# Another order of the seven products in both down projections, with half of one product's loads on the queue of the sums

## The chip, the core and the metric

The kernel runs on one core of one Trainium2 chip. The metric is device time in microseconds (us): the median of three runs of the kernel before is 1141.16 us (1140.47 to 1141.63). The profile is one execution, taken by the hardware profiler. Its engines are called PE (matrix multiply) and PEld (its weight load), DVE (VectorE), ACT (ScalarE), POOL (GpSimd) and SP (SyncE). SP, POOL and ACT also issue transfers (DMAs), which run on 16 DMA engines. Times inside the profile count from the start of its span.

## What is computed

The program is a two-layer decoder trunk on one sequence of 512 tokens with 1024 features, all in float32. Each layer is a mixer (attention in the first layer, a gated short convolution in the second) and a gated MLP, each behind an RMS norm and with a residual add. The change concerns the end of the MLP, its down projection:

```
SEQ = 512; D_MODEL = 1024; D_FF = 2816
def conv_ffn(h, norm_g, w_up, conv_w, w_down):
    xn = rms_norm(h, norm_g)
    u = causal_dwconv(xn @ w_up, conv_w)
    g, val = u[..., :D_FF], u[..., D_FF:]
    return (jax.nn.silu(g) * val) @ w_down
...
for layer in range(2):
    h = h + (attention_mixer(...) if layer == 0 else short_conv_mixer(...))
    h = h + conv_ffn(h, ffn_norm[layer], ffn_w_up[layer], ffn_conv[layer], ffn_w_down[layer])
```

So a down projection multiplies a 512 x 2816 matrix by a 2816 x 1024 matrix, once per layer.

## The kernel before

**The seven products.** `mlp` cuts the activations, the weights and the result of the down projection into two by two blocks and computes seven block products in place of eight. Their names are `p1 p7 p6 p2 q4 q5 p3`, and `PHASES` holds the order in which they run; this text calls them stage 1 to stage 7 by their place in it. One product runs over half of D_FF, which is 11 tiles of 128 rows. `GROUPS` cuts these into six chunks of 2, 2, 2, 1, 2 and 2 tiles. A chunk's weights are 512 KB, or 256 KB for the one of a single tile. One step of the program is one chunk, so a layer has 42 steps.

**Where a product's weights come from.** Two products take a block of the weights as it is: `p2` and `p3` load it into one of three buffers called `raw` (a plain load, on SP's queue). The other five take sums of blocks, and the additions are done by transfers. A transfer on POOL's queue with `accum_op` adds a block from memory to what lies in a tile. There are two chains of six tiles, one tile for each chunk:

- the first chain holds block (0,0) for `p1` (a plain load), and a later sum adds block (0,1) to it for `q5`;
- the second chain holds block (0,1) (a plain load), to which a first sum adds (1,1) for `p7`, a second adds (0,0) for `p6` and a third adds (1,0) for `q4`.

A sum may start only when the earlier content of its tile has been read. POOL issues its transfers in the order of the program, and while one waits, those behind it wait too. The tiles of the chains lie in tiles that the up projection has used, and carry their names: those of the first chain are `X_chain`, `Y_chain` and `p1_hi`/`p1_lo_chain`, those of the second `p7_hi`/`p7_lo_chain`, `q5_hi`/`q5_lo_chain` and `q4_hi`/`q4_lo_chain` for chunks 0 to 5. The number behind `chain` is the chunk, the next one the layer. The profile leaves leading numbers out and shows them as `p_hi_chain`, `q_lo_chain` and so on.

**The split.** A float32 product is made of three matmuls with a high and a low half of each factor. For each chunk ACT writes the high half of the weights (`whi`, L250) and DVE the low half (`wlo`, L251), each with three buffers. The same is done for the chunk's activations (`act`, L946 and L950 or L952). `weights` calls `fetch`, which loads and splits chunks two steps ahead of the one that PE works on; so a split is also held back by PE, which must have left the buffer of three chunks before. The load of a chunk on SP is issued as soon as its `raw` buffer is free.

**PE.** `step` does the matmuls of a chunk (L1505): 24 of 256 columns in the first layer and 12 of 512 columns in the second (half as many for the chunk of one tile), 132 and 66 in a stage. The accumulators A, T, R and B are two PSUM banks each; R starts as a negative copy of A.

**Other work of the stages.** DVE adds blocks of the activations in place for later products (L1407, L1409, L1411, from `operand`). `tasks` spreads adds into the residual (`join`, L1442), stores (`store`, L1447) and, in the first layer, the start of the next norm (`feed`) over the steps. The trailing slots of the up projection run in stage 1, and in the second layer the residual is transposed back in stages 2 and 3 (L1431).

Of the kernel before, what the change touches and what calls it, by code (L numbers as in the profile page):

```python
# [25 lines left out]
P = 128  # L26
# [27 lines left out]
def trunk(  # L54
# [158 lines left out]
    def want(dram, k0, nk, c0, n, *more):  # L213
        wanted.append((dram, k0, nk, (c0, n) + more))

    def want_sum(place, nk, n, *blocks):

        wanted.append((place, nk, n, blocks))

    def load(i):  # L220

        hi = wp.tile([P, CHUNK], F32R, tag="whi", name=f"whi{i}", bufs=3)
        lo = wp.tile([P, CHUNK], F32R, tag="wlo", name=f"wlo{i}", bufs=3)
        if callable(wanted[i][0]):
            place, nk, n, blocks = wanted[i]
            raw = place()
            if raw is None:
                raw = wp.tile([P, CHUNK], F32, tag="raw", name=f"raw{i}")
            v = raw[:, 0:nk * n].rearrange("p (k c) -> p k c", c=n)
            for (dram, k0, c0), fresh in blocks:  # L230
                src = dram[k0 * P:(k0 + nk) * P, c0:c0 + n].rearrange("(k p) c -> p k c", p=P)
                if fresh:
                    nc.sync.dma_start(v, src)
                else:
                    tc.keep_in_program_order(nc.gpsimd.dma_start(v, src, accum_op=ALU.add))
# [12 lines left out]
        def part(a, b):  # L248
            at_ = slice(a * n, b * n)
            return (act.activation(hi[:, at_], raw[:, at_], AF.Copy),  # L250
                    dve.tensor_tensor(lo[:, at_], raw[:, at_], f32(hi[:, at_]), op=ALU.subtract))  # L251
        halve[i] = part, nk
        return [t[:, 0:nk * n].rearrange("p (k c) -> p k c", c=n) for t in (hi, lo)]
# [37 lines left out]
    class Norm:  # L291
# [2 lines left out]

        def __init__(self, name, base):
            self.name, self.base = name, base
            self.row, self.held = None, []
            self.acc = own.tile([P, S], F32, tag="nrow", name=f"nacc_{name}", bufs=1) if name != "n0" else None

        def feed(self, f, src):  # L300
# [7 lines left out]
            dve.scalar_tensor_tensor(lo, src, g, f32(hi), op0=ALU.mult, op1=ALU.subtract)  # L308

        def squares(self, f, src):  # L310
            if f == 0:
# [118 lines left out]

    want_ffn(0, 2 * CLASSIC)

    def products(acc, w):
        for k in range(ND):
            yield mm3(acc, (w[0][:, k, :], w[1][:, k, :]), hs(k), k == 0, k == ND - 1)

    def project(acc, w):
        run(products(acc, w))
# [781 lines left out]
    def conv_seven(norm, mp):  # L1220
# [108 lines left out]
        accs = []  # L1329
        for j in range(8):  # L1330
            accs.append(bank("bbbbaabb"[j]))
            for _ in products(accs[-1], weights()):
                up.work_off(SHARE)
            if j in (1, 3):
                chores.append(input_(j // 2, *accs[j - 1:]))
            if j == 3:
                chores.append(prepare())
            if j >= 4:
                chores.insert(0, gate(j - 4, accs[j]))
            if j == 5:  # L1340
# [16 lines left out]
    def mlp(layer, norm, mp):  # L1357
        blocks, slots = up_seven(layer, norm, mp)
        acts, c1, c2 = {}, {}, {}
        PHASES = ("p1", "p7", "p6", "p2", "q4", "q5", "p3")  # L1360
        steps = [(p, g) for p in range(7) for g in range(len(GROUPS))]
        act_tags = [f"{n}_{i}" for n in ("p6", "p2") for i in ("hi", "lo")]

# [15 lines left out]
        def block(kh, ch, k0, fresh):  # L1379
            return (ffn_w_down[layer], kh * HF + k0, ch * 512), fresh  # L1380

        for name in PHASES:
# [14 lines left out]
        def operand(i):  # L1397
            if i >= len(steps):
                return
            p, g = steps[i]  # L1400
            k0, nk = GROUPS[g]
            name, sign = SOURCE[PHASES[p]]
            t = acts[i] = mp.tile([P, 2, 2, HT], F32R, tag=act_tags[i % 4], name=f"act{layer}_{i}")
            halves_to(t[:, 0, 0:nk, :], t[:, 1, 0:nk, :], blocks.block(name, k0, nk), sign)
            a, b, c, d = (blocks.block(n, k0, nk) for n in "abcd") if p in (1, 3, 4) else (None,) * 4
            if p == 1:
                dve.tensor_tensor(b, b, c, op=ALU.add)  # L1407
            elif p == 3:
                dve.tensor_tensor(a, b, a, op=ALU.subtract)  # L1409
            elif p == 4:  # L1410
                dve.tensor_tensor(b, b, d, op=ALU.add)  # L1411
# [8 lines left out]
        trail = slots[n_up:]  # L1420

        A, T, R, B = ([] for _ in range(4))
        home = {"p1": (A, "a", True), "p7": (T, "b", True), "p6": (R, "b", False), "p2": (A, None, False), "q5": (R, None, False),
                "p3": (B, "a", True), "q4": (T, None, False)}
        both, SUB = range(2), ALU.subtract
        kept = {}
# [17 lines left out]
        def store(i, ch, tb, acc, cuts=(0, 512)):  # L1444
# [6 lines left out]
        tasks = {  # L1451
            "p1": trail,
            "p7": [],
            "p6": [lambda b=b: join(1, 1, b, T[b], SUB) for b in both],
            "p2": [lambda b=b: join(1, 0, b, R[b], SUB) for b in both],
            "q4": [lambda b=b: done(0, 0, b, A[b]) for b in both],
            "q5": [lambda b=b: done(1, 0, b, T[b]) for b in both],
            "p3": [lambda b=b, fn=fn, i=i: fn(i, 1, b, R[b]) for b in both for fn, i in ((done, 1), (join, 0))],
        }
        after_ = None  # L1460
        if layer:
            residuals = [lambda q=q: residual_in(*q) for q in
                         ((1, 1, 0), (1, 1, 1), (1, 0, 0), (1, 0, 1), (0, 0, 0), (0, 0, 1), (0, 1, 0), (0, 1, 1))]
            tasks["p7"] += [None, None] + residuals[0:4]
            tasks["p6"] += residuals[4:]
        else:
            after_ = Norm("n2", 16)

            def feed(f):
                if f == 0:  # L1470
                    hs_open(1)
                after_.feed(f, h[:, f, :])
            tasks["q5"] += [lambda f=f: feed(f) for f in range(4)]

        def finish(b):
            if layer:
                store(0, 1, b, B[b], cuts=(0, 384, 512) if b else (0, 512))
                return
            join(0, 1, b, B[b])
            for f in (4 + 2 * b, 5 + 2 * b):  # L1480
                feed(f)

        todo = []
        for i, (p, g) in enumerate(steps):
            name, (k0, nk) = PHASES[p], GROUPS[g]
            acc, tag, fresh = home[name]
            if g == 0:
                todo.extend(tasks[name])
                if tag:
                    acc.extend(bank(tag) for _ in both)  # L1490
                if name == "p6":
                    for tb in both:
                        act.activation(R[tb], A[tb], AF.Copy, scale=-1.0)

# [14 lines left out]
            if i < late:  # L1509
# [78 lines left out]
```

## Time and profile before

| what | value |
|---|---|
| median of three runs | 1141.16 us |
| the profiled execution | 1140.43 us, its span 1138.5 us |
| mean granted clock of PE in the span | 0.998 |
| PE busy | 1123.4 us (99%) |
| DVE busy | 959.3 us (84%) |
| ACT busy | 669.3 us (59%) |
| POOL busy | 136.0 us (12%) |
| down projection of the first layer (L1505) | 504.09 to 621.29 us |
| down projection of the second layer (L1505) | 1017.11 to 1134.62 us |

A busy PE is not PE at its peak, since matmuls are pipelined; what tells of lost time is that the same number of matmuls takes longer in one stage than in another. Idle time of an engine that nobody waits for costs nothing. In the list of transfers a row gives the issue; the time to landing stands in a view of its own.

### The profile page before, as it was taken

To read this page: it belongs to the slowest core of one execution; us is meant where nothing else is said; L and a number is where in the kernel's file an instruction comes from. 1 tells how busy PE (TensorE), PEld (TensorE's weight loads), DVE (VectorE), ACT (ScalarE), POOL (GpSimd) and SP (SyncE) were. 2 spreads that over 40 slices of the span, in tenths; PEclk is the share of its full clock that TensorE was granted. 3 is DMA by queue.
4 is the path that set the end of the run, shared out by engine and by line. 5 is a ranking of instruction groups with operands and counts; after the bars stand their busy time and mean duration, and the time that the engine had idled before them with its cause. 6 is when DMAs were issued, how large, how long until landed. Compare 5 with 4: busy or idle time off the path is not lost.

```text
span 1138.5 us, 19066 instructions
## 1 busy us (share of the span) xinstructions
PE 1123.4 (99%) x7547; PEld 1006.6 (88%) x7547; DVE 959.3 (84%) x1453; ACT 669.3 (59%) x999; POOL 136.0 (12%) x150
## 2 busy tenths in 40 slices
PE   8999999999999999999999999999999999999998
PEld 6888787878889999999999899988889999998776
DVE  5787888887899899989788889865898898989775
ACT  7556576755545667676475455543445767676553
POOL 4000000000012111014400001000012111014400
PEclk9999999999999999999999999999999999999999
DMA  6412212022366877689944555543275867699952
GB/s 192 112 38 75 56 39 73 26 87 75 110 178 120 179 170 162 173 247 190 213 101 143 145 144 133 113 118 98 83 192 117 191 161 162 172 246 190 206 144 83
DMA packets 161080, 155.31 MB, mean 136 GB/s; under 512 B 6396, under 2 KB 136492, under 8 KB 160992
## 3 DMA queue, kind: packets, MB, share of 16 engines
q1 hardware_dynamic: 124256, 106.94, 30.6%
q0 software_dynamic: 36576, 47.10, 25.8%
q8 instruction: 59, 0.97, 0.3%
q14 instruction: 29, 0.24, 0.1%
q10 hardware_dynamic: 160, 0.07, 0.0%
HBM read 149.10 MB, written 2.10 MB: 133 GB/s over the span
## 4 chain that ended last, share of the span: by engine, by line
PE 86%; DVE 8%; DMA 2%; ACT 2%; issue 1%; SPq 0%; DVEq 0%; ACTq 0%
PE psb L997 25%; PE psa L997 10%; PE psb L1505 10%; PE psb L271 6%; PE psb L272 6%; PE psb L273 6%; PE psa L1505 5%; PE psa L273 4%; PE psa L272 4%; PE psa L271 4%; DVE wlo L251 2%; DMA raw<-in_ffn_w_down 2%; PE psb L645 1%; PE psa L741 1%; DVE rest L686 1%
## 5 line engine op out<-in xcount | busy, mean ns | idle before, releaser
L250 ACT ACTIVATE whi<-raw 128x1024 fp32r<-128x1024 f32 (+2 forms) x97 | 100.0, 1033 | 110.2 <-PE psb L272 32.0
L251 DVE TENSOR_TENSOR wlo<-raw,whi 128x1024 fp32r<-128x1024 f32 (+2 forms) x97 | 115.2, 1189 | 41.4 <-ACT whi L250 39.4
L997 PE MATMUL psb<-p_hi,wlo_p 128*128 128x256 f32 x384 | 108.3, 282 | 0.6 <-DVE wlo_p L950 0.6
L997 PE MATMUL psb<-p_lo,whi_p 128*128 128x256 f32 x384 | 108.1, 281 | 0.0
L997 PE MATMUL psb<-p_hi,whi_p 128*128 128x256 f32 x384 | 107.8, 281 | 0.0
L271 PE MATMUL psb<-hs_a,whi 128*128 128x512 f32 x256 | 104.6, 409 | 0.0
L273 PE MATMUL psb<-hs_a,wlo 128*128 128x512 f32 x256 | 101.3, 397 | 0.0
L997 PEld LDWEIGHTS psb<-p_hi,wlo_p 128*128 128x128 f32 x384 | 72.2, 188 | 0.8 <-DVE wlo_p L950 0.8
L997 PEld LDWEIGHTS psb<-p_hi,whi_p 128*128 128x128 f32 x384 | 72.8, 190 | 0.0
L997 PEld LDWEIGHTS psb<-p_lo,whi_p 128*128 128x128 f32 x384 | 72.2, 188 | 0.0
L997 PE MATMUL psa<-p_lo,whi_p 128*128 128x256 f32 x256 | 72.0, 281 | 0.0
L997 PE MATMUL psb<-q_hi,whi_q 128*128 128x256 f32 x256 | 72.0, 281 | 0.0
L997 PE MATMUL psb<-q_lo,whi_q 128*128 128x256 f32 x256 | 72.0, 281 | 0.0
L997 PE MATMUL psb<-q_hi,wlo_q 128*128 128x256 f32 x256 | 72.0, 281 | 0.0
L997 PE MATMUL psa<-p_hi,wlo_p 128*128 128x256 f32 x256 | 72.0, 281 | 0.0
L997 PE MATMUL psa<-p_hi,whi_p 128*128 128x256 f32 x256 | 71.8, 281 | 0.0
L1505 PE MATMUL psb<-act,whi 128*128 128x256 f32 x352 | 63.0, 282 | 0.4 <-DVE act L950 0.4
L380 DVE SCALAR_TENSOR_TENSOR uv<-yv,taps,uv 128x511 f32<-128x511 f32 (+1 forms) x88 | 62.5, 745 | 0.2
L380 DVE SCALAR_TENSOR_TENSOR ug<-yg,taps,ug 128x511 f32<-128x511 f32 (+1 forms) x88 | 62.0, 743 | 0.3 <-ACT ug L377 0.3
L271 PEld LDWEIGHTS psb<-hs_a,whi 128*128 128x128 f32 x256 | 48.4, 189 | 10.7 <-issue 1.2
L273 PEld LDWEIGHTS psb<-hs_a,wlo 128*128 128x128 f32 x256 | 48.1, 188 | 10.9
L1505 PE MATMUL psb<-whi,act 128*128 128x512 f32 x176 | 57.4, 399 | 0.1
(453 smaller groups left out, 3654.9 us busy)
## 6 DMA issues: line engine op xcount, KB each, us to landing
raw<-in_attn_w_in SPq DMA_DIRECT2D x24, 512.0 KB, 4.0
raw<-in_ffn_w_up SPq DMA_DIRECT2D x24, 512.0 KB, 3.9
raw<-in_ffn_w_down SPq DMA_DIRECT2D x20, 512.0 KB, 8.1
X<-in_ffn_w_up SPq DMA_DIRECT2D x16, 512.0 KB, 4.7
W<-in_ffn_w_up SPq DMA_DIRECT2D x16, 512.0 KB, 6.7
Y<-in_ffn_w_up SPq DMA_DIRECT2D x16, 512.0 KB, 4.6
Z<-in_ffn_w_up SPq DMA_DIRECT2D x16, 512.0 KB, 4.9
Y<-in_ffn_w_up POOLq DMA_DIRECT2D x16, 512.0 KB, 9.8
```

The costliest lines, as they stand in the source:

```text
L250: return (act.activation(hi[:, at_], raw[:, at_], AF.Copy), dve.tensor_tensor(lo[:, at_], raw[:, at_], f32(hi[:, at_]), op=ALU.subtract))
L251: dve.tensor_tensor(lo[:, at_], raw[:, at_], f32(hi[:, at_]), op=ALU.subtract))
L271: made = [pe.matmul(acc, w[0], rhs[0], start=first, stop=False), pe.matmul(acc, w[0], rhs[1], start=False, stop=False), pe.matmul(acc, w[1 ...
L272: pe.matmul(acc, w[0], rhs[1], start=False, stop=False),
L273: pe.matmul(acc, w[1], rhs[0], start=False, stop=last)]
L380: dve.scalar_tensor_tensor(dst[:, d:], src[:, 0:S - d], tap(j), dst[:, d:], op0=ALU.mult, op1=ALU.add)
L645: pe.matmul(ss[e][:, c:c + wide], ql[rows, b * P:n], kl[rows, 0:wide], start=first and b == bs[0], stop=last and b == bs[-1])
L686: dve.tensor_tensor_scan(back, back, begin[:, S - n:S][:, ::-1], 0.0, op0=ALU.mult, op1=ALU.max)
L741: pe.matmul(out_, w, t[:, first:first + step * (NB - k - 1) + 1:step, :], start=k == 0 and i == 0, stop=k == NB - 1 and i == 1)
L997: pe.matmul(to, w[a][:, k, c], x[b][:, k, :], start=fresh and i + k + t == 0, stop=i == 1 and k == 3 and t == 2, skip_group_check=not fresh)
L1505: pe.matmul(to, l, r, start=begin and o + t == 0, stop=end and t == 2 and o == (0 if layer else 1), skip_group_check=not fresh)
```

## The change

Three things change in both layers.

1. The order of the products becomes `p1 p7 p2 p6 p3 q5 q4`. The plain product `p2` becomes stage 3 and `p3` stage 5; `p6` becomes stage 4, `q5` stays stage 6 and `q4` becomes stage 7. The chains, the accumulators, the residual adds, the stores and the sums of activations are moved accordingly: the first layer now finishes features 4 to 7 of 8 before 0 to 3, and the projection that follows it runs over them in that order. The in-place sums of the activations are asked for three steps later (`sums`).
2. The sums for `p6` are issued in stage 2, ten steps before `fetch` would issue them: after each step of stage 2 the new `bring` issues the second sum of that step's chunk.
3. Of the six loads of `p2`, those of chunks 3, 4 and 5 are issued on POOL's queue (without `accum_op`) in place of SP's.

```
-    def want_sum(place, nk, n, *blocks):
+    def want_sum(place, nk, n, *blocks, queue=None):
...
+    def bring(i):
+        place, nk, n, blocks, queue = wanted[i]
...
+            if not fresh or queue:
+                tc.keep_in_program_order(
+                    nc.gpsimd.dma_start(v, src, **({} if fresh else {"accum_op": ALU.add})))
+            else:
+                nc.sync.dma_start(v, src)
...
-    def products(acc, w):
-        for k in range(ND):
+    def products(acc, w, order=tuple(range(ND))):
+        for k in order:
...
-            for _ in products(accs[-1], weights()):
+            for _ in products(accs[-1], weights(), (4, 5, 6, 7, 0, 1, 2, 3)):
...
-        PHASES = ("p1", "p7", "p6", "p2", "q4", "q5", "p3")
+        PHASES = ("p1", "p7", "p2", "p6", "p3", "q5", "q4")
...
-                    want_sum(lambda: None, nk, 512, block(1, 0 if name == "p2" else 1, k0, True))
+                    want_sum(lambda: None, nk, 512, block(1, 0 if name == "p2" else 1, k0, True), queue=pool if name == "p2" and g > 2 else None)
...
-            "q5": [lambda b=b: done(1, 0, b, T[b]) for b in both],
-            "p3": [lambda b=b, fn=fn, i=i: fn(i, 1, b, R[b]) for b in both for fn, i in ((done, 1), (join, 0))],
...
+            "q5": [lambda b=b: join(0, 1, b, B[b]) for b in both],
+            "q4": [lambda b=b, i=i: done(i, 1, b, R[b]) for b in both for i in (1, 0)],
...
-            tasks["q5"] += [lambda f=f: feed(f) for f in range(4)]
+            tasks["q4"] += [lambda f=f: feed(f) for f in range(4, ND)]
...
                 operand(i + 2)
-                left = (6 if name != "p3" else late - i) - (g if name != "p3" else 0)
+                sums(i + 2 - 3)
+                if name == "p7":
+                    j = begun + i + 2 * len(GROUPS)
+                    brought[j] = bring(j)
+                left = (6 if name != "q4" else late - i) - (g if name != "q4" else 0)
```

On POOL's queue, first layer, the sums of the second chain stood like this before, from chunk 2 of stage 2 on: four sums for `p7`, then the six for `p6` (`p7_hi_chain0` again is chunk 0 of `p6`), then the six for `q4`, of which two are shown.

```order
L235 DMA q5_hi_chain2_0_6046<-in_ffn_w_down 128x2x512
L235 DMA q5_lo_chain3_0_6081<-in_ffn_w_down 128x512
L235 DMA q4_hi_chain4_0_6116<-in_ffn_w_down 128x2x512
L235 DMA q4_lo_chain5_0_6151<-in_ffn_w_down 128x2x512
L235 DMA p7_hi_chain0_0_5969<-in_ffn_w_down 128x2x512
L235 DMA p7_lo_chain1_0_6007<-in_ffn_w_down 128x2x512
L235 DMA q5_hi_chain2_0_6046<-in_ffn_w_down 128x2x512
L235 DMA q5_lo_chain3_0_6081<-in_ffn_w_down 128x512
L235 DMA q4_hi_chain4_0_6116<-in_ffn_w_down 128x2x512
L235 DMA q4_lo_chain5_0_6151<-in_ffn_w_down 128x2x512
L235 DMA p7_hi_chain0_0_5969<-in_ffn_w_down 128x2x512
L235 DMA p7_lo_chain1_0_6007<-in_ffn_w_down 128x2x512
```

On the same queue at the same place, after the change:

```order
L232 DMA q5_hi_chain2_0_6048<-in_ffn_w_down 128x2x512
L232 DMA p7_hi_chain0_0_5969<-in_ffn_w_down 128x2x512
L232 DMA q5_lo_chain3_0_6083<-in_ffn_w_down 128x512
L232 DMA p7_lo_chain1_0_6006<-in_ffn_w_down 128x2x512
L232 DMA q4_hi_chain4_0_6119<-in_ffn_w_down 128x2x512
L232 DMA q5_hi_chain2_0_6048<-in_ffn_w_down 128x2x512
L232 DMA q4_lo_chain5_0_6155<-in_ffn_w_down 128x2x512
L232 DMA q5_lo_chain3_0_6083<-in_ffn_w_down 128x512
L232 DMA q4_hi_chain4_0_6119<-in_ffn_w_down 128x2x512
L232 DMA q4_lo_chain5_0_6155<-in_ffn_w_down 128x2x512
L232 DMA raw59_6284<-in_ffn_w_down 128x512
L232 DMA raw60_6319<-in_ffn_w_down 128x2x512
```

The sums of chunks 0, 1 and 2 for `p6` now stand between those of chunks 3, 4 and 5 for `p7`, which before stood ahead of all of them; and behind the six sums for `p6` come the three loads of `p2` (`raw59` to `raw61`; the last is not shown), then the sums for `q5` and those for `q4`.

On SP's queue, first layer, before: chunks 2 to 5 of `p2`, then the six of `p3`.

```order
L233 DMA raw64_6428<-in_ffn_w_down 128x2x512
L233 DMA raw65_6463<-in_ffn_w_down 128x512
L233 DMA raw66_6498<-in_ffn_w_down 128x2x512
L233 DMA raw67_6532<-in_ffn_w_down 128x2x512
L233 DMA raw80_6934<-in_ffn_w_down 128x2x512
L233 DMA raw81_6972<-in_ffn_w_down 128x2x512
```

On SP's queue at the same place, after the change: chunk 2 of `p2`, then the six of `p3`.

```order
L234 DMA raw58_6249<-in_ffn_w_down 128x2x512
L234 DMA raw68_6557<-in_ffn_w_down 128x2x512
L234 DMA raw69_6591<-in_ffn_w_down 128x2x512
L234 DMA raw70_6627<-in_ffn_w_down 128x2x512
L234 DMA raw71_6662<-in_ffn_w_down 128x512
L234 DMA raw72_6696<-in_ffn_w_down 128x2x512
```

The loads of chunks 3 to 5 of `p2` have left this queue, and those of `p3` follow directly on chunk 2; a load waits here only for its `raw` buffer.

More of the change, by code (lines that the diff above doesn't have):

```diff
@@ L214, in want @@
         wanted.append((dram, k0, nk, (c0, n) + more))
-    def want_sum(place, nk, n, *blocks):
-        wanted.append((place, nk, n, blocks))
+    def want_sum(place, nk, n, *blocks, queue=None):
+        wanted.append((place, nk, n, blocks, queue))
+    brought = {}
+    def bring(i):
+        place, nk, n, blocks, queue = wanted[i]
+        raw = place()
+        if raw is None:
+            raw = wp.tile([P, CHUNK], F32, tag="raw", name=f"raw{i}")
+        v = raw[:, 0:nk * n].rearrange("p (k c) -> p k c", c=n)
+        for (dram, k0, c0), fresh in blocks:
+            src = dram[k0 * P:(k0 + nk) * P, c0:c0 + n].rearrange("(k p) c -> p k c", p=P)
+            if not fresh or queue:
[3 more added lines that the diff above has]
+                nc.sync.dma_start(v, src)
+        return raw
     def load(i):
@@ L224, in load @@
         if callable(wanted[i][0]):
[L225 to L235, printed above, removed]
+            nk, n = wanted[i][1:3]
+            raw = brought.pop(i) if i in brought else bring(i)
         else:
@@ L296, in __init__ @@
             self.name, self.base = name, base
-            self.row, self.held = None, []
+            self.row, self.held, self.first = None, [], True
             self.acc = own.tile([P, S], F32, tag="nrow", name=f"nacc_{name}", bufs=1) if name != "n0" else None
@@ L310, in squares @@
         def squares(self, f, src):
-            if f == 0:
+            if self.first:
+                self.first = False
                 act.activation(self.acc, src, AF.Square)
@@ L431, in trunk @@
     want_ffn(0, 2 * CLASSIC)
-    def products(acc, w):
-        for k in range(ND):
-            yield mm3(acc, (w[0][:, k, :], w[1][:, k, :]), hs(k), k == 0, k == ND - 1)
+    def products(acc, w, order=tuple(range(ND))):
+        for k in order:
+            yield mm3(acc, (w[0][:, k, :], w[1][:, k, :]), hs(k), k == order[0], k == order[-1])
     def project(acc, w):
@@ L1380, in block @@
             return (ffn_w_down[layer], kh * HF + k0, ch * 512), fresh
+        begun = len(wanted)
         for name in PHASES:
@@ L1404, in operand, with sums @@
             halves_to(t[:, 0, 0:nk, :], t[:, 1, 0:nk, :], blocks.block(name, k0, nk), sign)
[L1405 to L1411, printed above, removed]
+        def sums(i):
+            if i >= len(steps):
+                return
+            p, g = steps[i]
+            if p in (1, 2, 3):
+                a, b, c, d = (blocks.block(n, *GROUPS[g]) for n in "abcd")
+                if p == 1:
+                    dve.tensor_tensor(b, b, c, op=ALU.add)
+                elif p == 2:
+                    dve.tensor_tensor(a, b, a, op=ALU.subtract)
+                else:
+                    dve.tensor_tensor(b, b, d, op=ALU.add)
         n_up = 7 * (HF - CLASSIC)
@@ L1422, in mlp @@
         A, T, R, B = ([] for _ in range(4))
-        home = {"p1": (A, "a", True), "p7": (T, "b", True), "p6": (R, "b", False), "p2": (A, None, False), "q5": (R, None, False),
+        home = {"p1": (A, "a", True), "p7": (T, "b", True), "p6": (R, None, False), "p2": (A, None, False), "q5": (R, None, False),
                 "p3": (B, "a", True), "q4": (T, None, False)}
@@ L1453, in mlp @@
             "p7": [],
-            "p6": [lambda b=b: join(1, 1, b, T[b], SUB) for b in both],
-            "p2": [lambda b=b: join(1, 0, b, R[b], SUB) for b in both],
-            "q4": [lambda b=b: done(0, 0, b, A[b]) for b in both],
-            "q5": [lambda b=b: done(1, 0, b, T[b]) for b in both],
-            "p3": [lambda b=b, fn=fn, i=i: fn(i, 1, b, R[b]) for b in both for fn, i in ((done, 1), (join, 0))],
+            "p2": [lambda b=b: join(1, 1, b, T[b], SUB) for b in both],
+            "p6": [lambda b=b: done(0, 0, b, A[b]) for b in both],
+            "p3": [lambda b=b: join(1, 0, b, R[b], SUB) for b in both],
+            "q5": [lambda b=b: join(0, 1, b, B[b]) for b in both],
+            "q4": [lambda b=b, i=i: done(i, 1, b, R[b]) for b in both for i in (1, 0)],
         }
@@ L1462, in mlp @@
             residuals = [lambda q=q: residual_in(*q) for q in
-                         ((1, 1, 0), (1, 1, 1), (1, 0, 0), (1, 0, 1), (0, 0, 0), (0, 0, 1), (0, 1, 0), (0, 1, 1))]
+                         ((1, 1, 0), (1, 1, 1), (0, 0, 0), (0, 0, 1), (1, 0, 0), (1, 0, 1), (0, 1, 0), (0, 1, 1))]
             tasks["p7"] += [None, None] + residuals[0:4]
-            tasks["p6"] += residuals[4:]
+            tasks["p2"] += residuals[4:]
         else:
@@ L1469, in feed @@
             def feed(f):
-                if f == 0:
+                if f == 4:
                     hs_open(1)
                 after_.feed(f, h[:, f, :])
-            tasks["q5"] += [lambda f=f: feed(f) for f in range(4)]
+            tasks["q4"] += [lambda f=f: feed(f) for f in range(4, ND)]
         def finish(b):
             if layer:
-                store(0, 1, b, B[b], cuts=(0, 384, 512) if b else (0, 512))
+                store(1, 0, b, T[b], cuts=(0, 384, 512) if b else (0, 512))
                 return
-            join(0, 1, b, B[b])
-            for f in (4 + 2 * b, 5 + 2 * b):
+            join(1, 0, b, T[b])
+            for f in (2 * b, 1 + 2 * b):
                 feed(f)
@@ L1490, in mlp @@
                     acc.extend(bank(tag) for _ in both)
-                if name == "p6":
+                if name == "p7":
+                    R.extend(bank("b") for _ in both)
                     for tb in both:
@@ L1513, in mlp @@
                 operand(i + 2)
-                left = (6 if name != "p3" else late - i) - (g if name != "p3" else 0)
+                sums(i + 2 - 3)
+                if name == "p7":
+                    j = begun + i + 2 * len(GROUPS)
+                    brought[j] = bring(j)
+                left = (6 if name != "q4" else late - i) - (g if name != "q4" else 0)
                 for _ in range(max(1, -(-len(todo) // max(left, 1))) if name != "p1" else 1):
```

## The prediction

> **What bounds the kernel now.** I read the page first (busy shares, chain), then each stage of the two down projections in the view of windows, then PE's pauses, the chain and the transfers there.
>
> ```profile
> PE 1123.4 (99%) x7547; PEld 1006.6 (88%) x7547; DVE 959.3 (84%) x1453; ACT 669.3 (59%) x999; POOL 136.0 (12%) x150
> PE 86%; DVE 8%; DMA 2%; ACT 2%; issue 1%; SPq 0%; DVEq 0%; ACTq 0%
> ```
>
> PE bounds almost everything, so only time in which PE waits can be won. The matmuls of L1505 by stage, first layer (stages 2 to 5), then second layer (2, 4, 5):
>
> ```profile
> 522.97:539.48 16.51, 16.07 (x134) 15.77 (x133) 1.00 1.04 172
> 539.48:555.10 15.62, 15.62 (x135) 15.62 (x133) 1.00 1.07 185
> 555.10:574.23 19.13, 17.68 (x134) 17.26 (x133) 0.91 1.09 247
> 574.23:589.84 15.61, 15.61 (x134) 15.61 (x133) 1.00 0.43 101
> ...
> 1035.31:1052.95 17.64, 16.80 (x67) 11.90 (x66) 1.00 1.05 180
> 1070.10:1088.33 18.23, 16.49 (x67) 12.32 (x68) 1.00 1.09 247
> 1088.33:1103.72 15.39, 15.39 (x68) 12.39 (x67) 1.00 0.40 116
> ```
>
> Columns: window, its length, PE and PEld busy, granted clock, DMA share, GB/s. A stage without waits takes 15.61 us, in the second layer 15.39. Stage 4 (`p2`) loses 19.13 - 15.61 = 3.5 us and 18.23 - 15.39 = 2.8 us. The DMA share says where from: over 1 up to stage 4, under 0.5 in stage 5. PE's pauses in stage 4, the chain of each layer there, and the clock:
>
> ```profile
> 565.91 0.51 PE L1505 MATMUL psa<-act,whi 128*128 128x256 f32 x2 [0.70 <-ACT whi L250]
> 567.16 0.39 PE L1505 MATMUL psa<-act,wlo 128*128 128x256 f32 x1 [0.75 <-DVE wlo L251]
> ...
> 1081.61 0.50 PE L1505 MATMUL psa<-wlo,act 128*128 128x512 f32 x1 [0.76 <-DVE wlo L251]
> 1085.67 0.50 PE L1505 MATMUL psa<-wlo,act 128*128 128x512 f32 x1 [0.76 <-DVE wlo L251]
> ...
> 555.86 8.83 DMA raw<-in_ffn_w_down
> ...
> 1072.29 10.90 DMA raw<-in_ffn_w_down
> ...
> 560.00:570.00 10.00, 8.55 (x60) 8.13 (x60) 3.26 (x5) 3.97 (x6) 0.38 (x1) 0.88 1.09 251
> 1080.00:1090.00 10.00, 8.26 (x33) 5.90 (x33) 7.44 (x9) 6.71 (x10) 0.00 (x0) 1.00 1.10 264
> ```
>
> A plain load takes 8.8 and 10.9 us there, because POOL has issued a crowd of sums (q0) beside it (q1). The same load took 4.2 us alone. Transfers from 553 to 583 us (two queue rows, and the last sum of `q5`, issued at 556.3 and so landing at 582.6), the lone load of 511.50, q0 alone from 538 to 549, and q0 over the whole first projection:
>
> ```profile
> q0 software_dynamic: 1963, 3.76, 69.2%
> q1 hardware_dynamic: 1504, 2.88, 29.7%
> p_lo_chain<-in_ffn_w_down POOLq DMA_DIRECT2D x1, 512.0 KB, 26.3
> ...
> DMA to landing us min/median/max: 4.2/4.2/4.2
> ...
> q0 software_dynamic: 1105, 2.13, 111.9%
> ...
> q0 software_dynamic: 6544, 12.06, 49.2%
> ```
>
> 2.13 MB in 11 us is 2.7 us for each 512 KB sum (0.524 MB), while q0 was never empty. The plain load is cheaper: 29.7% of 30 us for 2.88 MB is 1.6 us. Over the whole projection (145 us) a sum cost 49.2% x 145 / 23 = 3.1 us.
>
> **The change part by part.** *Stage 2, where POOL's order matters.* POOL's issues before:
>
> ```profile
> 512.97 1.41 POOL L235 DMA_DIRECT2D q_lo_chain<-in_ffn_w_down  x1
> 514.91 1.20 POOL L235 DMA_DIRECT2D q_hi_chain<-in_ffn_w_down  x1 [0.53 <-DMA q_hi_chain<-in_ffn_w_down]
> 515.62 1.73 POOL L235 DMA_DIRECT2D q_lo_chain<-in_ffn_w_down  x1
> 521.87 1.20 POOL L235 DMA_DIRECT2D p_hi_chain<-in_ffn_w_down  x1 [4.52 <-DVE wlo L251]
> 525.65 1.20 POOL L235 DMA_DIRECT2D p_lo_chain<-in_ffn_w_down  x1 [2.58 <-DVE wlo L251]
> 529.19 1.20 POOL L235 DMA_DIRECT2D q_hi_chain<-in_ffn_w_down  x1 [2.34 <-DVE wlo L251]
> ...
> 1034.29 1.20 POOL L235 DMA_DIRECT2D p_hi_chain<-in_ffn_w_down  x1 [4.64 <-DVE wlo L251]
> ...
> 528.92 1.06 ACT L250 ACTIVATE whi<-q_hi_chain 128x1024 fp32r<-128x1024 f32 x1 [1.86 <-PE psb L1505]
> 531.89 1.22 DVE L251 TENSOR_TENSOR wlo<-q_hi_chain,whi 128x1024 fp32r<-128x1024 f32 x1
> ...
> DMA to landing us min/median/max: 5.8/5.8/5.8
> ```
>
> The last row is the sum issued at 529.19. The sums of chunks 3, 4 and 5 of `p7` left at 512.97, 514.91 and 515.62, before stage 2 began. The next three are those of `p6`, each waiting for DVE to split that chunk of `p7`. After the change they stand between: chunk 3 of `p7` cannot leave before the split at 521.87, chunk 5 not before that at 529.19. So from 521.87 six transfers (5.5 x 512 KB) follow each other, and the last is chunk 5 of `p7`. All are issued by 530, before their turn, so the queue sets the pace: 521.87 + 5.8 + 4.5 x 2.7 = 539.8. The split adds 1.06 + 1.22 + 0.1 = 2.4 (542.2), the 22 of 24 matmuls that need the low half 22 x 15.61 / 132 = 2.6: stage 2 ends at 544.8 in place of 539.5, +5.3 us. Second layer: 1034.29 + 5.8 + 12.15 + 2.4 = 1054.6, then 10 of 12 matmuls (2.3) and four transposes:
>
> ```profile
> 1061.60 0.44 PE psc L1431 x4
> ```
>
> This gives 1057.4 against 1052.95, +4.4. Both together are 9 s - 14.6 for s us per sum. With s at a plain load's 1.6 it is about 0, with 3.1 it is +13.3; I take 2.7, measured on the same sums with q0 alone, as it will be here: SP issues nothing between 511.5 and 553.5.
>
> ```profile
> 511.50 0.37 SPq L233 DMA_DIRECT2D raw<-in_ffn_w_down  x1
> ...
> 553.52 5.64 SPq L233 DMA_DIRECT2D raw<-in_ffn_w_down  x3
> ```
>
> What waits behind: chunk 4's sum lands at 534.4 and holds PE about 3 us, but that lies within the wait for chunk 5. ACT and DVE stand too, with the splits of stage 3 behind, which still end (543.6) before PE asks (544.8).
>
> *Stage 3 (`p2`).* Chunks 0 to 2 are in place, loaded as before. Chunks 3 to 5 now follow the sums of `p6` on POOL. The last of these leaves at 542.3 and lands at 548.1; the loads leave as the splits of chunks 0 to 2 end (about 544, 547 and 550) and need 4.2 to 5 us: 549, 551, 555. PE asks for them at 553.3, 554.7 and 557.6, less a split of 1.4 to 2.4 us. That fits with 0 to 3 us to spare: cost 0, at most +1 a layer. So the stall of `p2` goes: -3.5 and -2.8, together -6.3.
>
> *Stage 5 (`p3`) is late next.* Its chunks 0 to 2 load from about 551, in time; 3 to 5 wait on SP for the splits of 0 to 2, as those of `p2` did. In stage 4 before they left 1.6 us ahead of the stage's start (553.52 against 555.10); here I count about 1 us earlier in each layer, since DVE has fewer sums in the way. But q0 is as full: behind 548 come 11 sums (29.7 us) and eight loads (13 us), to about 590, and stage 5 runs from 576 to 592; before, q0 was full to 582.6 with stage 4 ending at 574.2. So most of the stall comes back: 6.3 less 2 x 1 is +4.4. Bounds: 0 if the sums have thinned out, +6.3 if all returns.
>
> *Clock.* In the first layer two pauses of 0.70 and 0.75 us brought the granted clock to 0.88 over 10 us, in the second none did (1.00). Stage 2 will have pauses of up to 3 us. A slow clock after chunk 4 only fills the wait for chunk 5, so I take 0, with +1.5 a layer as the upper bound (16 matmuls at half speed, 0.095 us more each, as behind 567.16). The Trainium skill (TensorE: Matmul & The Clock Gate, section HAM oscillation) says that the clock halves where PE is idle for more than about 3.4 us. By that rule the clock would hold here and the sum stands; the trace of before does not agree, as it lost clock with 1.45 us of pauses.
>
> *Free.* Sums of activations (same number, VectorE idle 7 of 19 us in stage 4), R's copy one stage earlier (behind A's end, as before), residual transposes and stores (same number), the last products' weights (landed a stage ahead), the norm's features 4 to 7 first and the next projection in that order:
>
> ```profile
> 555.10:574.23 19.13, 17.68 (x134) 17.26 (x133) 12.10 (x16) 8.62 (x12) 5.28 (x5) 0.91 1.09 247
> 610.00:622.00 12.00, 12.00 (x100) 11.74 (x99) 6.81 (x9) 6.12 (x9) 0.00 (x0) 1.00 0.54 163
> ```
>
> DVE and ACT have 5 us to spare there for the four features that now come later (about 2.4 us on each); without it, up to +1.
>
> **Sum.** +5.3 + 4.4 - 6.3 + 4.4 = +7.8 us. On the profiled execution's own 1140.43 that is 1148.2; the median lies 0.7 higher, so 1148.9.
>
> **Rivals.** *Stage 5 is free.* POOL's later start lets its queue run dry, or the loads leave early enough: +9.7 - 6.3 = +3.4, 1144.6. For it: stage 5's loads of 3 to 5 leave earlier; against it: the 11 sums.
>
> *Faster: stage 2 isn't held.* If sums that follow each other closely need less than 2.7 us, 9 s - 14.6 shrinks. With stage 5 as forecast the change wins below s = 1.8, with stage 5 free below 2.3; at 1.6 the times are 1139.3 and 1134.9. For it: a plain load costs 1.6. Against it: 2.7 with q0 alone, and the share of 111.9%.
>
> *The queue brings nothing.* POOL's loads could be as late as SP's: stage 3 would keep the stall, +9.7 + 4.4 = +14.1, 1155.3. Against it: they stand ahead of the crowd, not beside it. The Trainium skill (DMA: Bandwidth & Descriptors, section Issuing engines are not separate DMA queues) says so in general: whoever issues, the transfers interleave on the same 16 engines. The trace agrees (8.8 us beside the sums, 4.2 alone).
>
> **How the numbers follow.** Forecast 0.51; stage 5 free 0.19; stage 2 not held 0.22, two thirds of it faster; the queue brings nothing 0.08. The forecast's own range is 1145.5 to 1152.5. 1138 to 1154 leaves out the fastest part of the third case and most of the last. 0.2% is 2.3 us, about what a measurement tells from no change. Faster 0.15, within it 0.08, slower 0.77.
>
> **What would show it.** Stage 2 near 21.8 and 22 us with pauses behind splits whose sum came late; stage 3 near its clean length; stage 5 1 to 3 us over; POOL waiting on DVE between two sums of `p7`. I am wrong if stage 2 keeps its length, or if the loss lies at the layer's end.

## The result, and the profile after

The changed kernel takes 1148.76 us (median of four runs, 1148.32 to 1149.60) against 1141.38 us for the kernel before on the same chip (four runs): a ratio of 1.0070, 95% interval 1.0054 to 1.0086. It is slower by about 7.4 us. The profiled execution took 1148.77 us, its span 1147.0.

The page of the changed kernel, busy time and chain. PE does the same 7547 matmuls; the chain holds 4% of DMA where it held 2%:

```profile
PE 1126.7 (98%) x7547; PEld 1009.6 (88%) x7547; DVE 960.7 (84%) x1453; ACT 669.4 (58%) x999; POOL 139.4 (12%) x156
PE 84%; DVE 8%; DMA 4%; ACT 2%; issue 1%; POOL 0%; DVEq 0%; ACTq 0%
```

The stages, in the same view of windows as in the prediction (window, length, PE and PEld busy, granted clock, DMA share, GB/s), now for the matmuls of L1522: stages 2 to 5 of the first layer, then of the second.

```profile
523.88:546.74 22.86, 18.04 (x134) 17.30 (x133) 0.93 0.97 165
546.74:562.41 15.67, 15.67 (x134) 15.67 (x133) 1.00 0.91 206
562.41:578.09 15.68, 15.68 (x134) 15.68 (x133) 1.00 1.12 231
578.09:595.05 16.96, 16.22 (x134) 15.80 (x133) 1.00 1.11 250
...
1040.34:1062.19 21.85, 18.35 (x68) 13.22 (x67) 0.92 0.99 171
1062.19:1079.33 17.14, 16.37 (x66) 12.10 (x67) 1.00 0.95 230
1079.33:1094.81 15.48, 15.48 (x67) 12.48 (x67) 1.00 1.12 237
1094.81:1111.89 17.08, 16.05 (x67) 12.24 (x66) 1.00 0.88 197
```

Stage 2 went from 16.51 to 22.86 us and from 17.64 to 21.85. The stage of `p2` is clean in both layers: stage 3 takes 15.67 us in the first layer, and in the second its 17.14 us are those that stage 3 took before (1052.95 to 1070.10, it holds the transposes), while stage 4 fell from 18.23 to 15.48. Stage 5 is 1.35 and 1.69 us over its clean length.

POOL's timeline in stage 2 of the first layer, what ACT's splits of chunks 4 and 5 waited for, and the first issue and the last split in the second layer:

```profile
522.76 1.20 POOL L232 DMA_DIRECT2D p_hi_chain<-in_ffn_w_down  x1 [8.41 <-DVE wlo L259]
523.50 1.41 POOL L232 DMA_DIRECT2D q_lo_chain<-in_ffn_w_down  x1
526.54 1.20 POOL L232 DMA_DIRECT2D p_lo_chain<-in_ffn_w_down  x1 [1.64 <-DVE wlo L259]
527.25 1.73 POOL L232 DMA_DIRECT2D q_hi_chain<-in_ffn_w_down  x1
529.49 1.20 POOL L232 DMA_DIRECT2D q_hi_chain<-in_ffn_w_down  x1 [0.50 <-DVE wlo L259]
530.21 2.65 POOL L232 DMA_DIRECT2D q_lo_chain<-in_ffn_w_down  x2
...
536.58 1.06 ACT L258 ACTIVATE whi<-q_hi_chain 128x1024 fp32r<-128x1024 f32 x1 [5.51 <-DMA q_hi_chain<-in_ffn_w_down]
541.65 1.06 ACT L258 ACTIVATE whi<-q_lo_chain 128x1024 fp32r<-128x1024 f32 x1 [3.49 <-DMA q_lo_chain<-in_ffn_w_down]
...
1038.14 1.20 POOL L232 DMA_DIRECT2D p_hi_chain<-in_ffn_w_down  x1 [8.16 <-DVE wlo L259]
...
1056.80 1.06 ACT L258 ACTIVATE whi<-q_lo_chain 128x1024 fp32r<-128x1024 f32 x1 [3.01 <-DMA q_lo_chain<-in_ffn_w_down]
```

POOL sits 8.4 us behind DVE's split of chunk 0, then issues a sum for `p6` and one for `p7` in turn. The last sum of `p7` leaves at 530.2 where it left at 515.6 before, and its split cannot start before 541.65. PE's pauses there, and the clock in two windows:

```profile
537.69 0.50 PE L1522 MATMUL psb<-act,whi 128*128 128x256 f32 x2 [3.43 <-ACT whi L258]
538.95 0.58 PE L1522 MATMUL psb<-act,wlo 128*128 128x256 f32 x1 [0.76 <-DVE wlo L259]
544.02 0.39 PE L1522 MATMUL psb<-act,wlo 128*128 128x256 f32 x1 [0.64 <-DVE wlo L259]
...
1052.84 0.50 PE L1522 MATMUL psb<-whi,act 128*128 128x512 f32 x1 [1.80 <-ACT whi L258]
...
538.50:542.00 3.50, 3.05 (x14) 3.05 (x15) 1.60 (x3) 0.35 (x1) 1.20 (x1) 0.51 1.12 204
1053.90:1057.40 3.50, 3.30 (x8) 2.65 (x9) 2.29 (x5) 0.60 (x1) 1.22 (x1) 0.51 1.10 191
```

Behind the pause PE runs at half clock for some 3.4 us, on chunk 4.

### The profile page after: what moved, and what is told of

The parts are those of the page before. It is cut to its first block, busy times and chain, and to the rows that moved or that the text cites. A ratio compares the mean times of both kernels' runs of the same rounds, so it can differ in the third digit from the quotient of the medians.

```text
span 1147.0 us, 19068 instructions
## 1 busy us (share of the span) xinstructions
PE 1126.7 (98%) x7547; PEld 1009.6 (88%) x7547; DVE 960.7 (84%) x1453; ACT 669.4 (58%) x999; POOL 139.4 (12%) x156
## 4 chain that ended last, share of the span: by engine, by line
PE 84%; DVE 8%; DMA 4%; ACT 2%; issue 1%; POOL 0%; DVEq 0%; ACTq 0%
PE psb L1006 25%; PE psa L1006 10%; PE psb L1522 8%; PE psb L279 6%; PE psb L280 6%; PE psb L281 6%; PE psa L1522 5%; PE psa L281 4%; PE psa L280 3%; PE psa L279 3%; DVE wlo L259 2%; DMA q_lo_chain<-in_ffn_w_down 2%; DMA raw<-in_ffn_w_down 2%; PE psb L654 1%; PE psa L750 1%
## 5 line engine op out<-in xcount | busy, mean ns | idle before, releaser
L1522 PE MATMUL psb<-act,whi 128*128 128x256 f32 x352 | 64.5, 286 | 3.4 <-ACT whi L258 3.4
L1522 PE MATMUL psb<-whi,act 128*128 128x512 f32 x176 | 57.6, 404 | 1.8 <-ACT whi L258 1.8
L1522 PEld LDWEIGHTS psb<-act,whi 128*128 128x128 f32 x352 | 55.4, 193 | 3.8 <-ACT whi L258 3.6
```

The costliest lines, as they stand in the source:

```text
L1522: pe.matmul(to, l, r, start=begin and o + t == 0, stop=end and t == 2 and o == (0 if layer else 1), skip_group_check=not fresh)
```

## Experiments

Each was timed beside the kernel before on the same chip. All move only the order or the queue of transfers, but for the last, which moves sums of activations.

**The sums of `p6` behind all sums of `p7`.**

```
-                if name == "p7":
-                    j = begun + i + 2 * len(GROUPS)
-                    brought[j] = bring(j)
+                if name == "p7" and g >= 3:
+                    for c in range(4) if g == 3 else (g,):
+                        j = begun + 18 + c
+                        brought[j] = bring(j)
```

> The changed kernel, but the second sums of chunks 0 to 3 (for p6) are issued only in the fourth step of stage 2, behind all six sums of p7, as they stood before. Theory (the order on POOL's queue holds stage 2): chunks 3 to 5 of p7 are again issued before stage 2 begins, stage 2 goes from 22.9 and 21.9 us back to 16.5 and 17.6, stage 3 stays clean (15.7 and 17.1), stage 5 keeps its 1.4 and 1.7 us over. Time 1148.8 - 10.5 = 1138.3 us, faster than the kernel before. Rival (stage 2 is held by the sheer number of transfers of p6 and p7, or by ACT's and DVE's new order, and not by their order on POOL): stage 2 stays at 20 us or more, 1145 to 1149 us.

Measured: 1136.99 us against 1140.39, ratio 0.9971 (0.9960 to 0.9982). Stage 2 in both layers, stage 5 in the first, and POOL's issues of chunks 3 to 5 of `p7` with the first of `p6`:

```profile
523.34:540.28 16.94, 16.18 (x135) 15.83 (x133) 1.00 0.98 169
...
571.89:588.87 16.98, 16.20 (x135) 15.79 (x134) 1.00 1.11 254
...
1033.99:1050.92 16.93, 16.35 (x67) 12.10 (x67) 1.00 1.07 179
...
513.76 1.41 POOL L232 DMA_DIRECT2D q_lo_chain<-in_ffn_w_down  x1
515.66 1.20 POOL L232 DMA_DIRECT2D q_hi_chain<-in_ffn_w_down  x1 [0.48 <-issue]
516.37 1.73 POOL L232 DMA_DIRECT2D q_lo_chain<-in_ffn_w_down  x1
522.23 1.20 POOL L232 DMA_DIRECT2D p_hi_chain<-in_ffn_w_down  x1 [4.13 <-DVE wlo L259]
```

The same transfers, the same products, the same splits: only the place of three sums on POOL's queue differs in each layer, those of chunks 0 to 2 for `p6` (that of chunk 3 stood behind all sums of `p7` in the changed kernel too). Stage 2 gets 5.9 and 4.9 us shorter, stage 5 keeps its 1.4 us. So the order on that queue is the cause of the slow stage 2, and it alone turns a gain of 0.3% into a loss of 0.7%.

**Two sums in between instead of three.**

```
-                if name == "p7":
-                    j = begun + i + 2 * len(GROUPS)
+                if name in ("p7", "p2") and 7 <= i <= 12:
+                    j = begun + i - 1 + 2 * len(GROUPS)
                     brought[j] = bring(j)
```

> The changed kernel, but each sum for p6 is issued one step later: two of them (chunks 0 and 1) instead of three stand between sums of p7, and only ahead of chunks 4 and 5. Theory (queue time: the last sum of p7 lands where six transfers have followed on the split of chunk 0): in the first layer the transfers behind that split are p6 chunk 0, p7 chunk 4, p6 chunk 1, p7 chunk 5, so the last lands at 528.5 + 3 x 2.65 = 536.5 instead of 541.5; stage 2 is 1.1 us over its 16.5 us in the first layer and at its 17.6 us in the second; 1139.4 us. Rival (each sum in between costs the same): two thirds of the 10.5 us stay, 1145.3 us.

Measured: 1139.88 us, ratio 0.9994 (0.9985 to 1.0003). Stage 2 in both layers, and the split of chunk 5:

```profile
522.93:540.75 17.82, 16.30 (x135) 15.88 (x134) 1.00 1.06 188
...
1034.19:1052.97 18.78, 16.50 (x67) 12.10 (x67) 1.00 1.05 184
...
535.66 1.06 ACT L258 ACTIVATE whi<-q_lo_chain 128x1024 fp32r<-128x1024 f32 x1 [3.88 <-DMA q_lo_chain<-in_ffn_w_down]
```

Chunk 5's sum is there at 535.66, 536.5 was expected, and the first layer is 1.3 us over its 16.51. The second is 1.1 over its 17.64 where none was expected; the rival's even price (1145.3 us) is out. The price of a sum in between is not even: with three the stage is 6.3 and 4.2 us over, with two 1.3 and 1.1. The last sum has some slack to lose first: in the first experiment, where none is in between, the split of chunk 5 starts at 532.22 and waits for PE and not for its sum.

**All loads of `p2` on SP again.**

```
-   queue=pool if name == "p2" and g > 2 else None
+   queue=None
```

> The changed kernel, but all six loads of p2 on SP's queue again. Theory (the loads' place ahead of the sums makes stage 3 clean): POOL goes on with the sums for q5 at once, the loads run beside them and take 8 to 11 us instead of 4 to 5, stage 3 gets its 3.5 and 2.8 us back; the sums are over earlier, so stage 5 may lose its 3.0 us: 1152 to 1155 us. Rival (the new place of p2 in the order is what made it clean, the queue brings nothing): stage 3 stays at 15.7 and 15.5 (behind the transposes 17.1) us, time 1146 to 1149 us.

Measured: 1154.16 us, ratio 1.0122 (1.0108 to 1.0136). Stages 2, 3 and 5 of the first layer; POOL's first sums for `q5`, which now follow at once on those of `p6`; the landing of SP's loads of 546.7 and 549.6 (`p2`, chunks 4 and 5); PE's pause in stage 2 and the clock behind it:

```profile
522.02:545.33 23.31, 19.18 (x135) 18.50 (x133) 0.85 0.95 162
545.33:564.91 19.58, 16.56 (x134) 15.89 (x133) 1.00 1.08 242
...
580.53:596.41 15.88, 15.88 (x135) 15.68 (x133) 1.00 0.86 234
...
543.30 2.95 POOL L232 DMA_DIRECT2D X_chain<-in_ffn_w_down  x2
...
DMA to landing us min/median/max: 9.0/9.6/10.1
...
535.91 0.62 PE L1522 MATMUL psb<-act,whi 128*128 128x256 f32 x2 [3.49 <-ACT whi L258]
...
540.00:542.00 2.00, 2.00 (x11) 2.00 (x11) 0.95 (x1) 2.00 (x3) 0.00 (x0) 0.50 1.10 199
```

Stage 3 gets its stall back (19.58 - 15.67 = 3.9 us; in the second layer 19.24 - 17.14 = 2.1, and in `p6` behind it none). Stage 5 is 1.1 and 0.5 us shorter than with the loads on POOL. So it is the queue that makes `p2` clean and not its new place, and the price is paid by stage 5: a load on POOL keeps the sums behind it back, and what is kept back is in the way later.

**The kernel before, with only the loads of chunks 3 to 5 of `p2` on POOL.**

```
 PHASES = ("p1", "p7", "p6", "p2", "q4", "q5", "p3")
-                    want_sum(lambda: None, nk, 512, block(1, 0 if name == "p2" else 1, k0, True))
+                    want_sum(lambda: None, nk, 512, block(1, 0 if name == "p2" else 1, k0, True), queue=pool if name == "p2" and g > 2 else None)
```

(`want_sum` and `load` take the new argument as in the changed kernel; that part of the edit isn't shown.)

> The kernel before with its own order of products, only the loads of chunks 3 to 5 of p2 (stage 4) on POOL's queue. Theory (the queue alone takes p2's stall away, and the sums for q4 that now wait behind the loads still come in time): stage 4 goes from 19.1 and 18.2 us to 15.6 and 15.4, the rest stays: 1141.2 - 6.3 = 1134.9 us. Rival 1 (POOL, waiting for a buffer, brings the sums of q4 too late): stage 4 is clean and stage 5 is held 2 to 5 us a layer, 1139 to 1145 us. Rival 2 (the queue brings nothing): 1141.2 us.

Measured: 1141.19 us, ratio 1.0004 (0.9995 to 1.0013), no difference. Stages 4 and 5 of the first layer, POOL's first load and first sum for `q4`, and the split that waits for it:

```profile
554.63:570.41 15.78, 15.78 (x135) 15.63 (x133) 1.00 0.83 206
570.41:588.98 18.57, 16.51 (x134) 15.91 (x134) 1.00 1.12 219
...
553.26 0.60 POOL L234 DMA_DIRECT2D raw<-in_ffn_w_down  x1 [16.25 <-DVE wlo L252]
...
559.24 1.27 POOL L234 DMA_DIRECT2D p_hi_chain<-in_ffn_w_down  x1
...
569.30 1.06 ACT L251 ACTIVATE whi<-p_hi_chain 128x1024 fp32r<-128x1024 f32 x1 [4.04 <-DMA p_hi_chain<-in_ffn_w_down]
```

The first rival holds. `p2` is clean, but POOL waits 16 us with an empty queue for a `raw` buffer, the first sum of `q4` leaves at 559.2 and is there 10 us later, 1 us late for stage 5, and each of the next two is late by about as much again: 18.57 - 15.6 = 3.0 us. The second layer's stage 5 is 2.9 us over, and the first layer's stage 6 another 1.6. The theory left out that these sums run beside the loads of `p2` and `p3`: a sum alone lands in 5.8 us. The changed order earns its place here: its two stages behind `p2` need none of the sums that POOL holds back.

**No early sums for `p6` at all.** (The three lines with `bring` are left out of `mlp`; the sums go out behind `p2`'s loads on POOL.)

> The changed kernel without the early issue in stage 2: the sums for p6 leave behind p2's loads on POOL, from about 545 us on. Theory (only the order in stage 2 was wrong, and p6 has time): stage 2 at 16.5 to 16.9 us in both layers, stage 3 clean, p6's sums land at 551 to 564 and are wanted by 554 to 568: stage 4 clean; behind them the sums for q5 and q4 run until after stage 5, whose stall grows from 1.4 and 1.7 us to 3 to 4 a layer: 1137.0 + 2 to 5 = 1139 to 1142 us. Rival (p6's sums are late too): stage 4 is 2 to 4 us over in each layer as well, 1143 to 1148 us.

Measured: 1144.86 us, ratio 1.0037 (1.0025 to 1.0050). Stage 4 of the first layer:

```profile
555.28:574.37 19.09, 16.82 (x133) 16.06 (x133) 1.00 1.12 224
```

My theory missed it and the rival has it: stages 2 and 3 are clean (16.71 and 15.77 us in the first layer, 16.93 and 17.13 in the second), but stage 4 is 3.5 us over, as the first sum for `p6` leaves at 544.6 and takes 9.5 us beside `p3`'s loads; the second layer's stage 4 is 1.8 us over, a little less than the rival's 2, and stage 5 is 2.3 and 3.3 us over. So the early issue is needed; only its place was wrong.

**`p3`'s loads of chunks 3 to 5 on POOL as well,** with the order of the first experiment.

```
-   queue=pool if name == "p2" and g > 2 else None
+   queue=pool if g > 2 else None
```

> e1_sums_behind with the loads of chunks 3 to 5 of p3 (stage 5) on POOL's queue too, ahead of the sums for q5 and q4, which then leave only from about 575 us on. Theory (stage 5 is late because of the sums that run beside its loads): stage 5 goes from 17.0 and 17.1 us to 15.7 and 15.4; six sums from 575 on land at 582 to 595, 2.5 to 3 us ahead of need in stage 6, and those of q4 behind them likewise, so 1137.0 - 3.0 = 1134.0 us. Rival (as in e5_order_of_before, the sums held behind POOL's loads come too late): stage 5 is clean and stage 6 is 2 to 4 us over in each layer, 1138 to 1142 us.

Measured: 1138.51 us, ratio 0.9983 (0.9974 to 0.9992). Stages 5 and 7 of the first layer, and the landing of the three loads for the next projection (`conv_w_in`, pieces of 512 bytes) that SP issues from 575.0 on:

```profile
570.67:586.29 15.62, 15.62 (x135) 15.62 (x134) 1.00 0.80 178
...
602.41:621.95 19.54, 17.20 (x134) 15.96 (x132) 1.00 0.62 115
...
DMA to landing us min/median/max: 15.1/23.2/32.3
```

Half of it held: stage 5 is clean in both layers (15.62 and 15.40), and the second layer is clean to its end. But in the first, 12 sums and those loads share the engines, stage 6 is 0.5 us over and stage 7 is 3.7. The rival had expected such a hold in stage 6 and in both layers. That the strided loads are what makes the first layer differ from the second is argued; the next two runs change the sums' time as well.

**`p3` on POOL in the second layer only.** (The condition becomes `g > 2 and (name == "p2" or layer)`.)

> e4_p3_on_pool_too, but the loads of p3 stay on SP's queue in the first layer and go to POOL's in the second alone. Theory (the loss in the first layer's stage 7 came from the sums of q4 running beside the strided loads of the next projection, which the second layer has not): the first layer is as in e1_sums_behind (stage 5 1.4 over, stage 7 at 15.8), the second as in e4 (stage 5 at 15.4, 6 and 7 clean): 1.7 us below e1, 5.1 us below the kernel before, 1135.5 us if that stands at 1140.6. Rival (e4's loss was something else in the program): 1137 us or more.

Measured: 1134.51 us against 1141.14, ratio 0.9947 (0.9934 to 0.9959). Stage 5 takes 16.98 and 15.40 us, stage 7 15.82 and 15.51: each layer as expected. The time is 6.6 us below the kernel before, where 5.1 was expected.

**Three sums for `q5` ahead of `p3`'s loads,** with those on POOL in both layers:

```
+                if name == "p6" and g == 0:
+                    for c in range(3):
+                        j = begun + 30 + c
+                        brought[j] = bring(j)
```

> e4_p3_on_pool_too, but the first three sums for q5 are issued at the start of stage 4, in the time in which POOL's queue was empty there (551 to 568 us in the first layer). Theory (the sums of q5 and q4 were simply too many behind p3's loads): the crowd ends about 8 us earlier in the first layer, at 606 in place of 614, and chunk 3 of q4 lands at 600 in place of 608.5: stage 7 goes from 19.5 back to 15.8 us, stage 5 stays at 15.6 and 15.4: 3.0 us below e1, 6.4 below the kernel before, 1134.2 us if that stands at 1140.6. Rival (three sums beside p3's first loads make stage 5 late again): stage 5 0.5 to 1.5 us over, 1135.5 to 1137 us.

Measured: 1133.66 us, ratio 0.9936 (0.9922 to 0.9949). Stage 7 of the first layer:

```profile
601.63:617.52 15.89, 15.89 (x134) 15.72 (x132) 1.00 0.20 42
```

Every stage from 3 on is clean in both layers (stage 5 takes 15.68 and 15.40 us). The three sums left at 544.0 to 545.5 us, right behind `p2`'s loads and still in stage 3; the expectation had them leave in stage 4. This version beats both kernels: 0.64% below the kernel before, about 1.3% below the changed one (0.9936 / 1.0070).

**The sums of activations at once,** `sums(i + 2)` in place of `sums(i + 2 - 3)`, with the order of the first experiment.

> e1_sums_behind with the in-place sums of the activations asked for right behind their operand and not three steps later. Theory (they are free either way, VectorE idles 7 of 19 us in such a stage): 1137.0 us, within 0.2%. Rival (a sum ahead of a split on VectorE delays the low half): 18 sums a layer of 0.68 us, of which a few lie ahead of a late split, 1138.5 to 1140 us.

Measured: 1137.54 us against 1140.79, ratio 0.9972 (0.9962 to 0.9982), beside 0.9971 without it. They are free.

## Why the prediction was right

Predicted were +7.8 us and 1148.9; measured +7.4 and 1148.76. By its terms (stage lengths of the two profiled executions):

| term | predicted | measured |
|---|---|---|
| stage 2, first and second layer | +5.3 and +4.4 | +6.35 and +4.21 |
| stall of `p2` gone | -3.5 and -2.8 | -3.46 and -2.75 |
| stage 5 (`p3`), both layers | +4.4 | +1.35 + 1.69 = +3.0 |
| all else | 0 | +0.2 in the other stages |

The mechanism and the sign of each term hold. That the sum is nearer than its terms is in part luck: stage 2 was 0.9 us more than forecast and stage 5 1.4 us less, and the two errors cancel.

*Stage 2.* The mechanism is the forecast's: the `p7` sums stand behind `p6` sums that wait on DVE, and putting them back (1136.99 us) takes the loss away. From the first of the six sums to the split of the last it took 541.65 - 522.76 = 18.9 us, where 5.8 + 4.5 x 2.7 = 17.95 was counted. That is 2.9 us a sum and not 2.7. The queue was not always as full as the step said: the third sum left only at 526.54, behind its own split, and the traffic sank at 529 us, when the two sums ahead of it were nearly through.

```profile
529.00:530.00 1.00, 1.00 (x10) 0.96 (x9) 1.00 (x3) 0.08 (x1) 0.52 (x1) 1.00 0.76 98
...
534.00:540.00 6.00, 1.82 (x10) 1.41 (x9) 2.40 (x4) 1.58 (x2) 0.81 (x1) 0.88 1.13 206
```

At the 206 GB/s of the second row a sum of 0.524 MB takes 2.5 us, and from 529 to 534 some 0.25 MB less than that were moved: about 1.2 us, by my estimate. In the second layer the sums took nearly the same (1056.80 - 1038.14 = 18.7), but the first left 2.2 us before the stage began and not 1.0 as before, which made up for it; that this layer's +4.21 is so near to +4.4 is luck too. The rival that the hold is not there at all (s near 1.6 us) is out.

*Stage 3.* The loads on POOL took 4.3 to 4.9 us to land (4.2 to 5 counted), and the run with them on SP shows that without the queue the stall is there: 9.0 to 10.1 us to landing, and 1154.2 us, where the rival "the queue brings nothing" had 1155.3. Here the Trainium skill (DMA: Bandwidth & Descriptors, section Issuing engines are not separate DMA queues) and the trace agree on what shares the engines, but the rule gives the wrong forecast if read as "the queue is no matter": POOL's gain is that the sums wait behind the loads.

*Stage 5.* The sign was right and the size, 4.4, was 1.4 us too much, nearly all of it in the first layer (1.35 us, where 3.5 - 1 was counted; in the second 1.69, where it was 2.8 - 1). The term assumed that `p3`'s loads leave 1 us earlier in a layer than `p2`'s did and meet the same crowd. SP's issue, the landing of its three loads and the two splits that waited, and before them the split of chunk 5 of `p2` in the kernel before:

```profile
568.77 1.06 ACT L250 ACTIVATE whi<-raw 128x1024 fp32r<-128x1024 f32 x1 [2.39 <-DMA raw<-in_ffn_w_down]
...
575.14 5.83 SPq L234 DMA_DIRECT2D raw<-in_ffn_w_down  x3
...
DMA to landing us min/median/max: 6.2/8.3/9.3
...
586.10 1.06 ACT L258 ACTIVATE whi<-raw 128x1024 fp32r<-128x1024 f32 x1 [3.55 <-DMA raw<-in_ffn_w_down]
589.96 1.06 ACT L258 ACTIVATE whi<-raw 128x1024 fp32r<-128x1024 f32 x1 [2.28 <-DMA raw<-in_ffn_w_down]
```

The first left 2.95 us ahead of the stage (578.09), not 2.6, and the crowd cost a little less (8.3 us against 8.8). So chunk 5's split began 11.87 us into the stage, where it had been 13.67 in the kernel before (568.77 - 555.10): 1.8 us earlier and not 1. The other 0.37 us is time that the term took for waiting on loads and that was clock: from that split to the end of the stage it is 5.09 us now and was 5.46, when PE ran at half clock behind its pauses. Both make up the 2.17 us by which this stage is shorter than `p2`'s was. In the second layer, where neither stage lost clock, the split is 1.14 us earlier and the rest equal. The rival that stage 5 is free is out. That these sums are the cause is shown by the run that puts the loads ahead of them: stage 5 is then clean.

*Clock.* Both stages 2 ran 3.4 us at half clock, and it cost nothing, as forecast: in the first layer PE still waited for chunk 5's low half at 544.02, and from that chunk's split to the end of the stage it takes 5.09 us, as in stage 5 at full clock. That it can cost is seen in the run with `p2` on SP. There the half clock held from 536 to 543, PE came to chunk 5 only at 542, after its high half had been ready at 541, and from the split to the end it takes 5.37 us. (Stage 2 is 0.45 us longer than in the changed kernel, the other 0.17 being a later split. In the second layer it is 1.8 us longer, at 23.61, of which 1.2 come from the first sum for `p6`, which left 1.0 us ahead of the stage and not 2.2.)

*Free.* The next norm's order, residuals and stores cost nothing seen: stages 6 and 7 together differ by 0.1 us, and from the end of the first down projection to the start of the second it is 395.5 us after and 395.8 before.

What stays open is a remainder of 0.9 us in the profiles: the spans differ by 8.5 us, the stages by 7.6. The first down projection began at 505.0 us after and 504.1 before, with the same program ahead of it. In the nine experiments it began at 503.1 to 506.0, so this is the spread of a single execution.

## What to carry to other kernels

On a queue that issues in order, a transfer that must wait for a buffer delays everything behind it, so an early issue ("prefetch") belongs behind whatever is wanted sooner; here three sums in the wrong place in each layer cost over 10 us. A transfer that holds others back can also be of use: it keeps a crowd off the engines while urgent loads run, as long as what it holds back still lands in time. A lead alone doesn't tell whether it does: the first sum behind POOL's loads left 11 to 12 us ahead of its stage both in the kernel before with `p2` on POOL, where `p3`'s loads from SP ran beside it and the stage was 3.0 and 2.9 us over, and with `p3` on POOL, where no such loads did and it was 0.5 us over in one layer and clean in the other. Ask of each moved load not only when it lands, but what it lets through, and who needs that next.

## What was not expected of the hardware

Pauses of PE of under 2 us were followed by half clock in some places and not in others. In the kernel before it was 0.70 and 0.75 us (first layer; the clock was 0.51 from 567.5 to 571). In the changed kernel's second layer, pauses of 1.80 and 0.76 us with 0.5 us of work between were followed by 3.4 us at half clock. Three pauses of 0.76 us some 4 us apart (no early sums, stage 4) left it at 1.00, and so did pauses of 0.81 and 0.97 us in stage 7 of the run with `p3` on POOL and of 1.51 and 0.76 us in stage 3 of the run with `p2` on SP. After 3.49 and 0.64 us (`p2` on SP) it lasted over 6 us and not 3.4. The rule that the Trainium skill gives (TensorE: Matmul & The Clock Gate, section HAM oscillation: pauses over about 3.4 us) fits the first layer of the changed kernel, where the pause was 3.43, and not its second, nor the kernel before. What decides whether short pauses halve the clock, and between 3.4 and 6 us, no run here shows.
